# Turning V and A with VectorE and a scratch in HBM in place of TensorE, in a layer of attention, retention and a gated MLP

## The chip, the cores and the metric

The kernel runs on one core of a Trainium2 chip. The metric is the time of one launch on the device in microseconds (us), lower is better; runs are compared by their median. Engines are named as the profile names them: PE (TensorE, matmul), PEld (its weight load), DVE (VectorE), ACT (ScalarE), POOL (GpSimd) and SP (SyncE, which here issues the DMAs).

## What is computed

One layer over 256 tokens and 16 meta tokens (272 positions), 2048 wide, in float32. Cut to what matters:

```python
u = rmsnorm(h, attn_norm); proj = u @ w_in
aq, ak, av, rq, rk, rv, rg = split(proj)
# 8 attention heads: two score maps of 64 dims each, one V of 128 dims
p = softmax(q @ k.T * scale + alibi)            # for both maps
ya = (p[0] - lam * p[1]) @ av                    # A @ V
ya = rmsnorm(ya) * (1 - lam_init)
# 4 retention heads: q, k of 128 dims, V of 256 dims
yr = rmsnorm(retention(rq, rk, rv)) * silu(rg)
h = h + concat(ya, yr) @ w_out
u = rmsnorm(h, ffn_norm)
h = h + (silu(conv3(u @ w_gate)) * (u @ w_up)) @ w_down
out = rmsnorm(h)
```

Only the last 258 positions are needed as queries (3 blocks of 86, `QT`); keys come in blocks of 100, 86 and 86 (`KB`).

## The kernel before

**Tiling.** Activations lie transposed: features on the partitions, positions along the free axis. A projection of 128 features is one `gemm` (L262 to L303): 16 blocks of the contraction, three matmuls each, since weights and activations are split into a high and a low part (`whi`, `wlo`; `xhi`, `xlo`): whi with x high, whi with x low, wlo with x high (L292 to L294). That makes 48 matmuls of 258 columns (q) or 272 (k, v). An attention head is three gemms, q, k and v; a retention head is four for k, q and two halves of v, and two more for its gate.

**Weights.** A gemm's weights are one chunk of 1 MB. SP loads it into one of three buffers (`raw`, L95); ACT rounds each half of it into `whi` (L107) and DVE subtracts for `wlo` (L108), three buffers each. The next chunk is loaded into a buffer when both halves of its old chunk have been split. So the split of a chunk's second half on DVE sets when the load three chunks on is issued. SP's queue issues every DMA of this kernel's main part, in one order.

**Order.** What goes beside the gemms is a list of side tasks; `gemm` takes the next one from it (`pump`) after every quarter, every 12 matmuls. A head puts 12 tasks on the list when its gemms are written, so they run beside the gemms of the next head or the one after. The first four gemms take nothing, which leaves the list some tasks behind. Within that, the order on each engine is set by the framework's scheduler, which places instructions by its own estimate of times.

**An attention head's tasks** (`att_tasks`, L324). `scores(i)` for the three blocks of queries: four matmuls into the PSUM tile `sc`, the bias and row minimum on DVE, the exponentials on ACT, and on DVE the difference of the two maps, `A` (L367; queries on partitions, keys along the free axis). V comes out of its gemm with its features on the partitions. The value product needs keys on the partitions, of both: `vtr` (L372) turns V with 3 transposes on PE into `pv`, and DVE copies it to SBUF (`vt`, L376, L377); `atr` (L380) turns A with 6 into `pa`, and ACT and DVE copy it (`at`, L389). `av` (L393) is the value product (L398, 12 records in the trace), with its row norm; `ytr` (L408) turns the result back with PE.

**A retention head's tasks** (`ret_tasks`, L430). `scores`, then `vtr`, which turns both halves of V with 6 transposes on PE (`rv`, L456) and copies them on ACT (L459), then `av` (`ro`, L467), `stats` and `scale`.

**After that** comes the output projection (L569 to L591). There each of the 16 steps turns a tile in blocks of 32 x 32 on DVE (`hb`, L586) and stores it in four DMAs to a scratch in HBM (`hd`, L589), beside the load of a residual tile (`xres`, L571); later the rows are loaded from it. The MLP, two thirds of the kernel, follows.

Of the kernel before, what the change touches and what calls it, by code (L numbers as in the profile page):

```python
# [10 lines left out]
F32 = mybir.dt.float32  # L11
# [3 lines left out]
AF = mybir.ActivationFunctionType  # L15
ALU = mybir.AluOpType
# [3 lines left out]
P = 128  # L20
# [4 lines left out]
T = META + SEQ  # L25
Q0 = META - 2
NQ = T - Q0
QT = NQ // 3
TW = 288
XO = 32 - META  # L30
# [29 lines left out]
def trunk_kernel(ctx, tc, a, out):  # L60
    nc = tc.nc
# [90 lines left out]
    def misc(name):  # L152
        return ps1.tile([P, 512], F32, tag="misc", bufs=3, name=name)
# [145 lines left out]
    with ExitStack() as p1:  # L299
# [22 lines left out]
        late = []  # L322

        def att_tasks(h, q, k, v):  # L324
            slope = 2.0 ** (-(h + 1))
            tasks = []
            As = {}
            vt = ap_.tile([P, 3, P], F32, tag="vt", name=f"vt{h}")
# [10 lines left out]
            def scores(i):  # L339
                def f():  # L340
# [17 lines left out]
                    for m in range(2):  # L358
# [7 lines left out]
                    A = ap_.tile([QT, T], F32, tag="A", bufs=3, name=f"A{h}_{i}")  # L366
                    V.scalar_tensor_tensor(out=A[:, :nk], in0=e[:, 1, :nk], scalar=sm[:, 1:2],  # L367
                                           in1=e[:, 0, :nk], op0=ALU.mult, op1=ALU.add)
                    As[i] = A
                return f  # L370

            def vtr():  # L372
                ps = misc(f"pv{h}")
                for j, (b, e) in enumerate(KB):
                    PE.transpose(ps[:e - b, j * P:(j + 1) * P], v[:, b:e], idt)
                V.tensor_copy(out=vt[:KB[0][1], 0], in_=ps[:KB[0][1], :P])  # L376
                V.tensor_copy(out=vt[:QT, 1:3].rearrange("p a b -> p (a b)"),  # L377
                              in_=ps[:QT, P:3 * P])

            def atr():  # L380
                pa = [misc(f"pa{h}_0"), misc(f"pa{h}_1")]
                for j, (b, e) in enumerate(KB):
                    for i in range(j, 3):
                        c = (i - j) * QT + (j == 1) * NQ
                        PE.transpose(pa[j // 2][:e - b, c:c + QT], As[i][:, b:e],
                                     idt[:QT, :QT])
                for j, (b, e) in enumerate(KB):
                    c = (j == 1) * NQ
                    (V.tensor_copy if j else S.copy)(  # L389
                        out=at[j][:e - b].rearrange("p a b -> p (a b)"),  # L390
                        in_=pa[j // 2][:e - b, c:c + (3 - j) * QT])
# [25 lines left out]
            def turn():  # L417
                vtr()
                atr()

            def values():
                av()
                while late:
# [3 lines left out]
            return [prelude, scores(0), scores(1), nop, scores(2), nop, nop, turn,  # L427
                    nop, values, nop, nop]

        def ret_tasks(r, k, q, vs):  # L430
# [20 lines left out]
            def vtr():  # L451
                pv = [misc(f"rv{r}_0"), misc(f"rv{r}_1")]
                for j, (b, e) in enumerate(KB):
                    for c in range(2):
                        d = (j % 2) * 2 * P + c * P
                        PE.transpose(pv[j // 2][:e - b, d:d + P], vs[c][:, b:e], idt)  # L456
# [39 lines left out]
            return [scores, nop, vtr, nop, nop, av, nop, nop, stats, scale]  # L496
# [327 lines left out]
```

## Time and profile before

| | |
|---|---|
| median of 3 runs | 1181.58 us (1180.9 to 1181.71) |
| the profiled execution | 1180.86 us |
| its span in the profile | 1179.1 us |
| mean granted clock of PE | 0.998 of full speed |
| attention and retention stage | up to some 340 us of the span |

A row of groups in the profile reads: line, engine, operation, tile written <- tiles read, partitions x elements, type, count | busy us, mean ns of one | idle time of the engine ahead of them, and what ended it. A row of the timeline: start, duration, engine, line, operation. A row of waits: who waited <- for what: us in total, times, the longest. A row of the chain: start, duration, engine, line and count, of the chain of work that ended last. Names lose their numbers in these rows: `pa` stands for all heads' `pa5_0` and the like.

### The profile page before, as it was taken

To read this page: it belongs to the slowest core of one execution; us is meant where nothing else is said; L and a number is where in the kernel's file an instruction comes from. 1 tells how busy PE (TensorE), PEld (TensorE's weight loads), DVE (VectorE), ACT (ScalarE), POOL (GpSimd) and SP (SyncE) were. 2 spreads that over 40 slices of the span, in tenths; PEclk is the share of its full clock that TensorE was granted. 3 is DMA by queue.
4 is the path that set the end of the run, shared out by engine and by line. 5 is a ranking of instruction groups with operands and counts; after the bars stand their busy time and mean duration, and the time that the engine had idled before them with its cause. 6 is when DMAs were issued, how large, how long until landed. Compare 5 with 4: busy or idle time off the path is not lost.

```text
span 1179.1 us, 19921 instructions
## 1 busy us (share of the span) xinstructions
PE 1168.4 (99%) x8087; PEld 1094.0 (93%) x8087; DVE 803.1 (68%) x1442; ACT 561.6 (48%) x871; POOL 2.0 (0%) x7
## 2 busy tenths in 40 slices
PE   9999999999999999999999999999999999999997
PEld 8999999999999999999999999999999888888886
DVE  7898787766677677776767767677767645454544
ACT  7566665544444444444444444444444434343442
POOL 0000000000000000000000000000000000000000
PEclk9999999999999999999999999999999999999999
DMA  8543434445458776555555554455555655555552
GB/s 309 188 150 136 168 137 167 150 150 179 146 180 247 224 238 220 191 190 189 179 180 187 193 192 179 179 183 188 197 184 179 217 206 184 198 195 185 195 193 106
DMA packets 53661, 219.82 MB, mean 186 GB/s; under 512 B 21763, under 2 KB 26091, under 8 KB 28609
## 3 DMA queue, kind: packets, MB, share of 16 engines
q1 hardware_dynamic: 53280, 217.36, 52.7%
q8 instruction: 63, 1.03, 0.3%
q0 software_dynamic: 144, 1.05, 0.2%
q14 instruction: 30, 0.24, 0.1%
q10 hardware_dynamic: 144, 0.14, 0.0%
HBM read 214.34 MB, written 4.19 MB: 185 GB/s over the span
## 4 chain that ended last, share of the span: by engine, by line
PE 96%; DVE 2%; DMA 1%; issue 0%; ACT 0%; DVEq 0%; ACTq 0%
PE mm L292 17%; PE mm L293 17%; PE mm L294 17%; PE mm L288 14%; PE mm L290 7%; PE o L657 7%; PE o L658 7%; PE o L659 7%; PE po L398 1%; DMA raw<-in_w_in_dram 1%; PE ro L467 1%; DVE wlo L108 1%; PE mm L211 0%; PE mm L287 0%; PE mm L213 0%
## 5 line engine op out<-in xcount | busy, mean ns | idle before, releaser
L108 DVE TENSOR_TENSOR wlo<-raw,whi 128x1024 fp32r<-128x1024 f32 x381 | 466.2, 1224 | 244.2 <-ACT whi L107 239.0
L107 ACT CAST whi<-raw 128x1024 fp32r<-128x1024 f32 x381 | 400.1, 1051 | 480.8 <-PE mm L293 259.9
L288 PE MATMUL mm<-g,whi 128*128 128x512 f32 x704 | 249.1, 393 | 0.0
L293 PE MATMUL mm<-g,whi 128*128 128x258 f32 x704 | 199.9, 284 | 0.0
L292 PE MATMUL mm<-g,whi 128*128 128x258 f32 x704 | 199.5, 283 | 0.0
L292 PE MATMUL mm<-x,whi 128*128 128x272 f32 (+1 forms) x688 | 199.2, 290 | 0.0
L293 PE MATMUL mm<-x,whi 128*128 128x272 f32 (+1 forms) x688 | 198.9, 289 | 0.0
L294 PE MATMUL mm<-g,wlo 128*128 128x258 f32 x704 | 198.8, 282 | 0.0
L294 PE MATMUL mm<-x,wlo 128*128 128x272 f32 (+1 forms) x688 | 197.3, 287 | 1.1 <-DVE wlo L108 1.1
L290 PE MATMUL mm<-g,wlo 128*128 128x256 f32 x660 | 185.2, 281 | 0.0
L288 PEld LDWEIGHTS mm<-g,whi 128*128 128x128 f32 x704 | 132.1, 188 | 26.1
L293 PEld LDWEIGHTS mm<-g,whi 128*128 128x128 f32 x704 | 132.4, 188 | 1.9
L294 PEld LDWEIGHTS mm<-g,wlo 128*128 128x128 f32 x704 | 132.9, 189 | 0.0
L292 PEld LDWEIGHTS mm<-g,whi 128*128 128x128 f32 x704 | 132.5, 188 | 0.0
L294 PEld LDWEIGHTS mm<-x,wlo 128*128 128x128 f32 x688 | 129.7, 189 | 1.3 <-DVE wlo L108 1.3
L658 PE MATMUL o<-wlo,fhi 128*128 128x512 f32 x334 | 130.0, 389 | 0.0
L659 PE MATMUL o<-whi,flo 128*128 128x512 f32 x334 | 130.0, 389 | 0.0
L293 PEld LDWEIGHTS mm<-x,whi 128*128 128x128 f32 x688 | 129.8, 189 | 0.0
L292 PEld LDWEIGHTS mm<-x,whi 128*128 128x128 f32 x688 | 129.7, 188 | 0.0
L290 PEld LDWEIGHTS mm<-g,wlo 128*128 128x128 f32 x660 | 124.4, 189 | 0.0
L657 PE MATMUL o<-whi,fhi 128*128 128x512 f32 x334 | 117.0, 389 | 0.0
L659 PEld LDWEIGHTS o<-whi,flo 128*128 128x128 f32 x334 | 62.7, 188 | 13.0
(245 smaller groups left out, 1366.7 us busy)
## 6 DMA issues: line engine op xcount, KB each, us to landing
raw<-in_w_in_dram SPq DMA_DIRECT2D x44, 1024.0 KB, 4.7
raw<-in_w_gate_dram SPq DMA_DIRECT2D x44, 1024.0 KB
raw<-in_w_up_dram SPq DMA_DIRECT2D x44, 1024.0 KB, 4.8
raw<-in_w_down_dram SPq DMA_DIRECT2D x44, 1024.0 KB, 4.7
raw<-in_w_out_dram SPq DMA_DIRECT2D x16, 1024.0 KB, 4.8
raw<-in_w_first_dram SPq DMA_DIRECT2D x6, 512.0 KB
xres<-in_x_dram SPq DMA_DIRECT2D x16, 129.0 KB, 4.3
hd<-hb SPq DMA_DIRECT2D x64, 32.0 KB, 3.7
```

The source lines that it names most:

```text
L107: S.copy(out=hi, in_=src)
L108: V.tensor_tensor(out=lo, in0=src, in1=hi.bitcast(F32), op=ALU.subtract)
L288: PE.matmul(ps[:, :2 * n], wh, xb, start=(k == 0), stop=(k == KT - 1))
L290: PE.matmul(ps[:, :n], wl, xh, start=False, stop=False)
L292: PE.matmul(ps[:, :n], wh, xh, start=(k == 0), stop=False)
L293: PE.matmul(ps[:, :n], wh, xl, start=False, stop=False)
L294: PE.matmul(ps[:, :n], wl, xh, start=False, stop=(k == KT - 1))
L398: PE.matmul(ps[:QT, i * P:(i + 1) * P], at[j][:n, i - j], vt[:n, j], start=(j == 0), stop=(j == i))
L467: PE.matmul(y[:, c, j * QT:NQ], vt[:n, j, cs], sd[j][:n], start=(j == 0), stop=(j == 2))
L657: PE.matmul(o, ah, wh, start=start and kk == 0, stop=False)
L658: PE.matmul(o, ah, wl, start=False, stop=False)
L659: PE.matmul(o, al, wh, start=False, stop=stop and kk == 1)
```

## The change

V and A are no longer turned by PE. DVE transposes them in blocks of 32 x 32 into another tile, stores put these blocks in their turned places in a scratch in HBM, and loads fetch the turned matrix from there. V goes out in four stores (`hv`), a retention head's in eight (`rhv`), each of three blocks of A in three (`ha`; the last of the three only 22 columns wide, since a block has 86 queries); V comes back in two loads, A in three. A's and V's tiles are padded to whole blocks and their pads set to zero by POOL. The value product of a head, which was the tenth task of its own twelve, is put on `due` and runs in the fourth task of the next head's list, directly behind that head's second scores. In a retention head the loads stand in the second task, `av` in the eighth. One square on ACT of 2 x 258 takes the place of two. The tiles that this needs take the places of others (`g0`, `g1`, `k2`, `bias`).

The lines of the gemm move down by one (L293 to L295), the value product is L421 and the third split L109.

```diff
@@ -320,11 +321,31 @@
 
         nop = lambda: None
         late = []
-
-        def att_tasks(h, q, k, v):
+        due = []
+
+        def last_av():
+            while due:
+                due.pop()()
+
+
+        def turned(v, vb, hv, c):
+            V.transpose(out=vb, in_=v)
+            for i in range(4):
+                d = c * P + i * 32
+                nc.sync.dma_start(
+                    out=hv[:, d:d + 32].rearrange("(b t) f -> t b f", t=32),
+                    in_=vb[i * 32:(i + 1) * 32].rearrange("t (b f) -> t b f", f=32))
+
+        AW = (128, 192, TV)
+        Ab = [ap_.tile([96, AW[i]], F32, name=f"Ab{i}", bufs=1) for i in range(3)]
+        for A in Ab:
+            nc.gpsimd.memset(A, 0.0)
+
+        def att_tasks(h, q, k, hv):
             slope = 2.0 ** (-(h + 1))
             tasks = []
             As = {}
+            ha = dp.tile([TV, NQ], F32, name=f"ha{h}")
             vt = ap_.tile([P, 3, P], F32, tag="vt", name=f"vt{h}")
             at = [ap_.tile([P, 3 - j, QT], F32, tag=f"at{j}", name=f"at{h}_{j}")
                   for j in range(3)]
@@ -363,32 +384,34 @@
                     V.tensor_tensor(out=sm[:, 1:2], in0=sm[:, 1:2], in1=nlam[:QT], op=ALU.mult)
                     V.tensor_scalar(out=e[:, 0, :nk], in0=e[:, 0, :nk], scalar1=sm[:, 0:1],
                                     scalar2=None, op0=ALU.mult)
-                    A = ap_.tile([QT, T], F32, tag="A", bufs=3, name=f"A{h}_{i}")
-                    V.scalar_tensor_tensor(out=A[:, :nk], in0=e[:, 1, :nk], scalar=sm[:, 1:2],
-                                           in1=e[:, 0, :nk], op0=ALU.mult, op1=ALU.add)
-                    As[i] = A
+                    V.scalar_tensor_tensor(out=Ab[i][:QT, :nk], in0=e[:, 1, :nk],
+                                           scalar=sm[:, 1:2], in1=e[:, 0, :nk],
+                                           op0=ALU.mult, op1=ALU.add)
+                    As[i] = ap_.tile([P, TV], F32, tag="g1", name=f"A{h}_{i}")[:96, :AW[i]]
+                    V.transpose(out=As[i], in_=Ab[i])
                 return f
 
-            def vtr():
-                ps = misc(f"pv{h}")
+            def vload():
+                nc.sync.dma_start(out=vt[:KB[0][1], 0], in_=hv[:KB[0][1]])
+                nc.sync.dma_start(out=vt[:QT, 1:3],
+                                  in_=hv[KB[0][1]:T].rearrange("(a s) d -> s a d", s=QT))
+
+            def atr(i):
+                def f():
+                    for p in range(3):
+                        n = min(32, QT - 32 * p)
+                        c = i * QT + 32 * p
+                        nc.sync.dma_start(
+                            out=ha[:AW[i], c:c + n].rearrange("(b t) f -> t b f", t=32),
+                            in_=As[i][p * 32:p * 32 + 32].rearrange(
+                                "t (b f) -> t b f", f=32)[:, :, :n])
+                return f
+
+            def aload():
                 for j, (b, e) in enumerate(KB):
-                    PE.transpose(ps[:e - b, j * P:(j + 1) * P], v[:, b:e], idt)
-                V.tensor_copy(out=vt[:KB[0][1], 0], in_=ps[:KB[0][1], :P])
-                V.tensor_copy(out=vt[:QT, 1:3].rearrange("p a b -> p (a b)"),
-                              in_=ps[:QT, P:3 * P])
-
-            def atr():
-                pa = [misc(f"pa{h}_0"), misc(f"pa{h}_1")]
-                for j, (b, e) in enumerate(KB):
-                    for i in range(j, 3):
-                        c = (i - j) * QT + (j == 1) * NQ
-                        PE.transpose(pa[j // 2][:e - b, c:c + QT], As[i][:, b:e],
-                                     idt[:QT, :QT])
-                for j, (b, e) in enumerate(KB):
-                    c = (j == 1) * NQ
-                    (V.tensor_copy if j else S.copy)(
-                        out=at[j][:e - b].rearrange("p a b -> p (a b)"),
-                        in_=pa[j // 2][:e - b, c:c + (3 - j) * QT])
+                    nc.sync.dma_start(out=at[j][:e - b].rearrange("p a b -> p (a b)"),
+                                      in_=ha[b:e, j * QT:])
+                due.append(values)
 
             def av():
                 ps = misc(f"po{h}")
@@ -414,20 +437,16 @@
                                        in1=yhi[:, h].bitcast(F32), op0=ALU.mult,
                                        op1=ALU.subtract)
 
-            def turn():
-                vtr()
-                atr()
-
             def values():
                 av()
                 while late:
                     late.pop()()
                 late.append(ytr)
 
-            return [prelude, scores(0), scores(1), nop, scores(2), nop, nop, turn,
-                    nop, values, nop, nop]
-
-        def ret_tasks(r, k, q, vs):
+            return [prelude, scores(0), scores(1), last_av, scores(2), atr(0), atr(1), vload,
+                    atr(2), nop, nop, aload]
+
+        def ret_tasks(r, k, q, hv):
             dt_ = ap_.tile([P, 2, NQ], F32, tag="t", name=f"dk_{r}")
             nc.sync.dma_start(out=dt_[:KB[0][1], 0], in_=a["decay0"][r])
             nc.sync.dma_start(out=dt_[:QT, 1], in_=a["decay1"][r])
@@ -449,14 +468,9 @@
                                     in1=dk[j], op=ALU.mult)
 
             def vtr():
-                pv = [misc(f"rv{r}_0"), misc(f"rv{r}_1")]
-                for j, (b, e) in enumerate(KB):
-                    for c in range(2):
-                        d = (j % 2) * 2 * P + c * P
-                        PE.transpose(pv[j // 2][:e - b, d:d + P], vs[c][:, b:e], idt)
-                for j, (b, e) in enumerate(KB):
-                    d = (j % 2) * 2 * P
-                    S.copy(out=vt[:e - b, j], in_=pv[j // 2][:e - b, d:d + 2 * P])
+                nc.sync.dma_start(out=vt[:KB[0][1], 0], in_=hv[:KB[0][1]])
+                nc.sync.dma_start(out=vt[:QT, 1:3],
+                                  in_=hv[KB[0][1]:T].rearrange("(a s) d -> s a d", s=QT))
 
             def av():
                 y = st["y"] = ps1.tile([P, 2, 512], F32, tag="sc", bufs=1, name=f"ro{r}")
@@ -466,10 +480,9 @@
                         n = e - b
                         PE.matmul(y[:, c, j * QT:NQ], vt[:n, j, cs], sd[j][:n],
                                   start=(j == 0), stop=(j == 2))
-                for c in range(2):
-                    q_ = ap_.tile([P, NQ], F32, tag="A", bufs=3, name=f"rsq{r}_{c}")
-                    S.activation(out=q_, in_=y[:, c, :NQ], func=AF.Square)
-                    st[c] = q_
+                q_ = ap_.tile([P, 2, NQ], F32, tag="bias", bufs=1, name=f"rsq{r}")
+                S.activation(out=q_, in_=y[:, :, :NQ], func=AF.Square)
+                st[0], st[1] = q_[:, 0], q_[:, 1]
                 while late:
                     late.pop()()
 
@@ -493,7 +506,7 @@
                     V.tensor_tensor(out=t, in0=st["y"][:, c, :NQ], in1=st["r"], op=ALU.mult)
                     yn[r, c] = t
 
-            return [scores, nop, vtr, nop, nop, av, nop, nop, stats, scale]
+            return [scores, vtr, nop, nop, nop, nop, nop, av, nop, stats, scale]
 
         yn = {}
 
@@ -514,14 +527,17 @@
         for h in range(AH):
             q = ap_.tile([P, NQ], F32, tag="q", name=f"q{h}")
             k = ap_.tile([P, T], F32, tag="k", name=f"k{h}")
-            v = ap_.tile([P, T], F32, tag="v", name=f"v{h}")
+            v = ap_.tile([P, TV], F32, tag="v", name=f"v{h}")
+            nc.gpsimd.memset(v[:, T:], 0.0)
             ps = gemm(idx, xhi, xlo, Q0, NQ, 1)
             V.scalar_tensor_tensor(out=q, in0=ps[:, :NQ], scalar=0.125, in1=rq_,
                                    op0=ALU.mult, op1=ALU.mult)
             ps = gemm(idx + 1, xhi, xlo, 0, T, 1)
             V.tensor_tensor(out=k, in0=ps[:, :T], in1=rk_, op=ALU.mult)
             ps = gemm(idx + 2, xhi, xlo, 0, T, 1)
-            V.tensor_tensor(out=v, in0=ps[:, :T], in1=rk_, op=ALU.mult)
+            V.tensor_tensor(out=v[:, :T], in0=ps[:, :T], in1=rk_, op=ALU.mult)
+            hv = dp.tile([TV, P], F32, name=f"hv{h}")
+            turned(v, ap_.tile([P, TV], F32, tag="g0", name=f"vb{h}"), hv, 0)
             idx += 3
             q2 = ap_.tile([P, 2, NQ], F32R, tag="q2", name=f"q2_{h}")
             k2 = ap_.tile([P, 2, T], F32R, tag="k2", name=f"k2_{h}")
@@ -535,11 +551,12 @@
                 V.tensor_copy(out=k2[os, m], in_=k[hs])
                 V.tensor_tensor(out=kl[hs, m], in0=k[hs], in1=k2[hs, m].bitcast(F32),
                                 op=ALU.subtract)
-            side.extend(att_tasks(h, q2, (k2, kl), v))
+            side.extend(att_tasks(h, q2, (k2, kl), hv))
+        side.extend([nop, nop, nop, last_av])
         for kind, r in RSEQ:
             if kind == "g":
                 for c in range(2):
-                    g = ap_.tile([P, NQ], F32, tag=f"g{c}", name=f"rg{r}_{c}")
+                    g = ap_.tile([P, TV], F32, tag=f"g{c}", name=f"rg{r}_{c}")[:, :NQ]
                     ps = gemm(idx, xhi, xlo, Q0, NQ, 1)
                     V.tensor_tensor(out=g, in0=ps[:, :NQ], in1=rq_, op=ALU.mult)
                     S.activation(out=g, in_=g, func=AF.Silu)
@@ -552,14 +569,16 @@
             V.tensor_tensor(out=k, in0=ps[:, :T], in1=rk_, op=ALU.mult)
             ps = gemm(idx + 1, xhi, xlo, Q0, NQ, 1)
             V.tensor_tensor(out=q, in0=ps[:, :NQ], in1=rq_, op=ALU.mult)
-            vs = []
+            vb = ap_.tile([P, 2, TV], F32, tag="k2", name=f"rvb{r}")
+            hv = dp.tile([TV, 2 * P], F32, name=f"rhv{r}")
             for c in range(2):
-                v = ap_.tile([P, T], F32, tag="e" if c else "v", name=f"rv{r}_{c}")
+                v = ap_.tile([P, TV], F32, tag="e" if c else "v", name=f"rv{r}_{c}")
+                nc.gpsimd.memset(v[:, T:], 0.0)
                 ps = gemm(idx + 2 + c, xhi, xlo, 0, T, 1)
-                V.tensor_tensor(out=v, in0=ps[:, :T], in1=rk_, op=ALU.mult)
-                vs.append(v)
+                V.tensor_tensor(out=v[:, :T], in0=ps[:, :T], in1=rk_, op=ALU.mult)
+                turned(v, vb[:, c], hv, c)
             idx += 4
-            side.extend(ret_tasks(r, k, q, vs))
+            side.extend(ret_tasks(r, k, q, hv))
         pump(len(side))
 
         gs = [big.tile([P, 2, HK, TW], F32R, tag=f"act{i}", name=f"g{i}") for i in range(2)]
```

PE, head 5. `mm22` is head 7's k gemm, `sc6_1` the second scores of head 6, `py4` the turning back of head 4's result. Before, from the last matmuls ahead of the value product, and A's transposes further up:

```order
L385 MATMUL pa5_0_2279<-c_ident_444,A5_2_2201 100x86
L385 MATMUL pa5_0_2279<-c_ident_444,A5_1_2151 86x86
...
L294 MATMUL mm22_2370<-x1_72,wlo45_2303 128x272
L398 MATMUL po5_2318<-vt5_1931,at5_0_1932 86x128 x2
L411 MATMUL py4_2351<-c_ident_444,yo_4_1623 128x86 x3
L292 MATMUL mm22_2370<-x1_72,whi45_2302 128x272
```

Now:

```order
L293 MATMUL mm23_2500<-x0_71,whi46_2401 128x272
L366 MATMUL sc6_1_2480<-k2_6_2310,q2_6_2309 86x186
L368 MATMUL sc6_1_2480<-klz_466,q2_6_2309 86x186
L366 MATMUL sc6_1_2480<-k2_6_2310,q2_6_2309 86x186
L368 MATMUL sc6_1_2480<-klz_466,q2_6_2309 86x186
L421 MATMUL po5_2519<-vt5_2000,at5_0_2001 86x128 x2
L421 MATMUL po5_2519<-vt5_2000,at5_1_2002 86x128
L421 MATMUL po5_2519<-vt5_2000,at5_0_2001 86x128
```

The product stood in head 7's k gemm, ahead of head 6's first scores; it has moved behind head 6's second scores, into head 7's v gemm (`mm23`), and the transposes `pa5` are gone.

SP, the same place. Before, only weights stood there:

```order
L95 DMA raw24_2371<-in_w_in_dram 128x2048
L95 DMA raw25_2468<-in_w_in_dram 128x2048
L95 DMA raw26_2567<-in_w_in_dram 128x2048
L95 DMA raw27_2683<-in_w_in_dram 128x2048
L95 DMA raw28_2781<-in_w_in_dram 128x2048
```

Now (`hv6` is head 6's V, `ha5` and `at5` are head 5's A):

```order
L96 DMA raw24_2399<-in_w_in_dram 128x2048
L404 DMA ha5_1999<-A5_1_2175 32x6x32 x2
L404 DMA ha5_1999<-A5_1_2175 32x6x22
L335 DMA hv6_2302<-vb6_2303 32x9x32 x4
L96 DMA raw25_2501<-in_w_in_dram 128x2048
L395 DMA vt6_2322<-hv6_2302 100x128
L404 DMA ha5_1999<-A5_2_2265 32x9x32 x2
L404 DMA ha5_1999<-A5_2_2265 32x9x22
L396 DMA vt6_2322<-hv6_2302 86x2x128
L412 DMA at5_0_2001<-ha5_1999 100x258
L412 DMA at5_1_2002<-ha5_1999 86x172
L412 DMA at5_2_2003<-ha5_1999 86x86
```

Between two loads of weights stand now the stores and loads of V and A, on the one queue; the last block's stores are behind raw25 and behind a load that waits for hv6's stores.

DVE, between the split of raw22's first half (`wlo44`) and that of raw23's (`wlo46`), now:

```order
L109 TENSOR_TENSOR wlo44_2337<-raw22_2179,whi44_2336 128x1024
L134 SCALAR_TENSOR_TENSOR r3t_2215<-r3o_2216,ms4_2207 86x3
L332 STREAM_TRANSPOSE vb6_2303<-v6_2009 128x288
...
L109 TENSOR_TENSOR wlo45_2370<-raw22_2179,whi45_2369 128x1024
L387 SCALAR_TENSOR_TENSOR Ab2_471<-e5_2_2257,sm5_2_2258 86x272
L134 SCALAR_TENSOR_TENSOR r3t_2215<-r3o_2216,ms4_2207 86x3
L533 SCALAR_TENSOR_TENSOR q7_2329<-mm21_2333,rstd1_81 128x258
L391 STREAM_TRANSPOSE A5_2_2265<-Ab2_471 96x288
L135 TENSOR_TENSOR r3t_2215<-r3t_2215,r3o_2216 86x3
L109 TENSOR_TENSOR wlo46_2402<-raw23_2334,whi46_2401 128x1024
```

The transpose of V, which PE did, stands behind `wlo44`, and that of A's last block behind `wlo45` and the multiplication that ends head 7's q gemm.

More of the change, by code (lines that the diff above doesn't have):

```diff
@@ L29 @@
 TW = 288
+TV = 288
 XO = 32 - META
@@ L569, in trunk_kernel @@
         for j in range(KT):
-            xr = ap_.tile([P, NQ], F32, tag="g0", name=f"xres{j}")
+            xr = ap_.tile([P, TV], F32, tag="g0", name=f"xres{j}")[:, :NQ]
             nc.sync.dma_start(out=xr, in_=a["x"][:, j, Q0:T])
             ps = gemm(idx + j, yhi, ylo, 0, NQ, 1)
-            hT = ap_.tile([P, NQ], F32, tag="g1", name=f"hT{j}")
+            hT = ap_.tile([P, TV], F32, tag="g1", name=f"hT{j}")[:, :NQ]
             V.tensor_tensor(out=hT, in0=ps[:, :NQ], in1=xr, op=ALU.add)
```

## The prediction

> **What bounds the kernel now.** I read the page first: busy times of the engines, then who is waited for.
>
> ```profile
> PE 1168.4 (99%) x8087; PEld 1094.0 (93%) x8087; DVE 803.1 (68%) x1442; ACT 561.6 (48%) x871; POOL 2.0 (0%) x7
> ```
>
> TensorE (PE) is busy through the whole span of 1179.1 us. The view of waits, for PE alone, says in what it ever waits:
>
> ```profile
> PE psx L158 <- DVE warm L146: 1.6, 1, 1.6
> PE mm L294 <- DVE wlo L108: 1.1, 1, 1.1
> ```
>
> Twice: once at the start, once while the first heads are set up. So each matmul taken from PE's stream shortens the kernel by the time it holds the stream, and each wait put into the stream lengthens it. How long a matmul holds the stream is not its mean duration, because matmuls overlap. Four rows of the timeline, PE alone, give the step from one to the next:
>
> ```profile
> 89.46 0.28 PE L294 MATMUL mm<-x,wlo 128*128 128x258 f32 x1
> 93.81 0.29 PE L294 MATMUL mm<-x,wlo 128*128 128x258 f32 x1
> 93.94 0.28 PE L292 MATMUL mm<-x,whi 128*128 128x272 f32 x1
> 95.81 0.28 PE L292 MATMUL mm<-x,whi 128*128 128x272 f32 x1
> ```
>
> Between the first two lie 36 steps: 4.35/36 = 0.121 us each. Between the last two lie 15: 1.87/15 = 0.125 us. A matmul of 0.28 us holds the stream for less than half of that.
>
> **What is removed.** The transposes are these groups (lines by shape: count, then busy us and mean ns):
>
> ```profile
> L385 PE MATMUL pa<-c_ident,A 86*100 86x86 f32 x24 | 4.9, 238 | 0.0
> L375 PE MATMUL pv<-c_ident,v 128*86 128x128 f32 x16 | 3.0, 272 | 0.0
> L375 PE MATMUL pv<-c_ident,v 128*100 128x128 f32 x8 | 2.2, 272 | 0.0
> L385 PE MATMUL pa<-c_ident,A 86*86 86x86 f32 x24 | 3.2, 237 | 0.0
> L456 PE MATMUL rv<-c_ident,rv 128*86 128x128 f32 x16 | 2.6, 273 | 0.0
> L456 PE MATMUL rv<-c_ident,rv 128*100 128x128 f32 x8 | 1.5, 272 | 0.0
> ```
>
> That is 48 of A, 24 of V in the attention heads and 24 of V in the retention heads. The chain of waits (start, us) says what they hold of the stream:
>
> ```profile
> 78.15 0.33 PE pv L375 x3
> 100.45 0.45 PE pa L385 x6
> 249.21 0.66 PE rv L456 x6
> ```
>
> So 0.11 us for one of V and 0.075 for one of A: 48 x 0.075 + 24 x 0.11 + 24 x 0.11 = 3.6 + 2.64 + 2.64 = **8.9 us**. The sum of the six busy times, 17.4 us, would be wrong by the overlap.
>
> One place gives some back. The second wait of PE ends a chain over DVE:
>
> ```profile
> 52.11 0.29 DVE vt L376
> 52.75 1.24 DVE wlo L108
> 54.03 0.39 PE mm L294
> ```
>
> The copies of head 0's V (0.64 us from one start to the next row's) go, but one or two transposes of V on DVE come before that split, of about 0.5 us each (next part): up to 0.3 us more. And the three transposes of head 0's V stood before this wait, where their 0.33 us only makes PE wait longer. Off go 0.6: **-8.3 us** before any new wait.
>
> **What is added, beside other work.** DVE loses four copies in each head and gains four transposes. The nearest row of such a transpose is L586:
>
> ```profile
> L586 DVE STREAM_TRANSPOSE hb<-hT 128x256 f32<-128x256 f32 x16 | 7.1, 445 | 0.5
> L377 DVE COPY vt<-pv 86x256 f32<-86x256 f32 x8 | 3.3, 408 | 0.0
> L389 DVE COPY at<-pa 86x172 f32<-86x172 f32 x8 | 2.6, 325 | 0.2 <-ACT at L389 0.2
> L376 DVE COPY vt<-pv 100x128 f32<-100x128 f32 x8 | 2.3, 282 | 0.1
> L389 DVE COPY at<-pa 86x86 f32<-86x86 f32 x8 | 1.9, 242 | 2.2 <-PE pa L385 2.1
> ```
>
> By columns: V, 288 wide, 0.50; A, 128, 192 and 288 wide, 0.22 + 0.33 + 0.50; together 1.55 us against 0.408 + 0.325 + 0.282 + 0.242 = 1.26. DVE gets 0.3 us more to do in each head of some 21 us. The first of these windows is such a head (span; PE, PEld, DVE, ACT, POOL busy; clock, DMA share, GB/s):
>
> ```profile
> 151.00:172.00 21.00, 21.00 (x178) 21.00 (x178) 17.16 (x58) 13.25 (x33) 0.00 (x0) 1.00 0.42 152
> 360.00:380.00 20.00, 20.00 (x168) 20.00 (x167) 13.94 (x22) 10.22 (x15) 0.00 (x0) 1.00 0.74 215
> 500.00:600.00 100.00, 100.00 (x707) 94.05 (x706) 70.35 (x107) 45.96 (x62) 0.00 (x0) 1.00 0.53 189
> ```
>
> DVE's 17.2 us of 21 become 17.5: hidden, as long as the splits of the weights keep their lead. ACT and PSUM only get relief. The pads' memsets go to POOL, which is idle.
>
> DMA gets 13 stores and 5 loads per head, the stores in pieces of 128 B or less: 4 x 288 + 3 x 608 = 2976 pieces. The second window holds the same kind of store (hd, 256 pieces of 128 B each, four per 5.8 us, and xres); its share is 0.21 above the third window's, or 4.2 us of 16 engines in 20 us for some 3500 pieces: at most 0.019 us of one engine each. A head's new pieces so cost 2976 x 0.019/16 = 3.5 us, its share goes from 0.42 to about 0.6. Under a share of 0.74 weights still come on time. Nor do the weights get late here (rows in the next part): raw24, issued at 152.05, has landed by 156.8; raw22 is split from 154.18 on (wlo44), and the fourth split after it, the first of raw24, is at 169.48.
>
> **The new wait.** A's way to the value products was PE, PSUM and a copy; now it is store, completion, load, completion, all on SP's one queue. The order after shows what stands there: raw25, the first load of vt6 (which waits for hv6's stores), the three stores of A5_2, the other load of vt6, three loads at5. I place this on the old trace:
>
> ```profile
> 152.05 0.33 SPq L95 DMA_DIRECT2D raw<-in_w_in_dram  x1
> 152.94 0.29 PE L347 MATMUL sc<-klz,q 128*86 128x272 f32 x1
> 154.18 1.21 DVE L108 TENSOR_TENSOR wlo<-raw,whi 128x1024 fp32r<-128x1024 f32 x1
> 158.84 0.33 SPq L95 DMA_DIRECT2D raw<-in_w_in_dram  x1
> 159.46 0.43 DVE L519 SCALAR_TENSOR_TENSOR q<-mm,rstd 128x258 f32<-128x258 f32 x1 [0.65 <-PE mm L294]
> 169.48 1.21 DVE L108 TENSOR_TENSOR wlo<-raw,whi 128x1024 fp32r<-128x1024 f32 x1
> ```
>
> When PE needs it: from the last second-map score of head 5 (152.94) to the first value product the order after has 122 gemm matmuls (48 of 258 columns, 74 of 272) and 8 scores, 15.6 us by the steps above: 168.5. When A5_2 is there: its transpose stands behind q7's multiplication (159.46 + 0.43): 160.4. When hv6 is there: vb6's transpose stands behind wlo44 (154.18 + 1.21), so four stores go out from 155.9 to 157.7. What the stores and loads take is in the DMA rows:
>
> ```profile
> L589 SPq DMA_DIRECT2D hd<-hb x64: 302/442/1095, 348.3 to 432.8; - x64
> DMA to landing us min/median/max: 1.7/3.7/4.3
> raw<-in_w_in_dram SPq DMA_DIRECT2D x44, 1024.0 KB, 4.7
> xres<-in_x_dram SPq DMA_DIRECT2D x16, 129.0 KB, 4.3
> ```
>
> An issue holds the queue 0.44 us. A landing takes 1.7 us at least and 3.7 to 4.3 close behind a weight load (xres is issued about a microsecond behind one, and hd's stores after it). So three landings follow one another: hv6 (last issued at 157.3), A5_2's stores (the third issued 0.9 us behind the first), and at5.
> [...]
> - All at 4.3: 161.6, 162.9 + 4.3 = 167.2, + 4.3 = 171.5. PE waits 3.0 us, in each of 8 heads: 24 us.
> - By the nearest rows: hv6 and at5 have no weight load right ahead (about 2), A5_2's stores do (3.7): 159.3; A5_2 from 160.4, third at 161.3, landed 165.0; at5_0 at 167.5. A microsecond is left.
>
> I take the last, and 2 us in all for heads in which it does not hold: head 7's stores stand among the eight stores of the first retention head's V, which are 3.5 us of issue on the same queue.
>
> The retention heads' V makes the same trip with eight stores; its product stands six task slots (of 12 matmuls, some 1.5 us each) behind the loads, 9 us against a landing of 4.3 at most, so I put no wait there.
>
> [...]
>
> **The sum.** 1180.86 (the profiled execution; span 1179.1 and 1.8 around it) - 8.9 + 0.6 + 2.0 = 1174.6. The median of the runs shown, 1181.58, lies 0.7 above that execution, so I say **1175**. A measurement of this kernel tells about 0.2% from no change, here 1179.2 to 1183.9.
>
> **Rivals.**
> 1. *The round trip takes what PE gives.* All three landings at hd's median: hv6 161.0, stores from 161.4, third at 162.3, landed 166.0, at5_0 at 169.7: PE waits 1.2 us x 8 = 9.6; 1180.9 - 8.3 + 9.6 = 1182, no difference. For it speaks that 3.7 is the median of such stores; against it, that all of these had a weight load and xres ahead of them.
> 2. *Slower: PE waits for at in every head.* One mechanism, the landing of A's second trip, at the place po L421. It costs from 1.04 us per head on (8.3/8) all that was won, and from 1.33 it is slower by over 0.2%. With 4.3 for each landing it is 3.0 us: 1180.9 - 8.3 + 24 = 1196.5; half way, at 2 us, 1188.6. For it: the margin is a microsecond over three landings, and a head that waits shifts the next one's work with it, so the wait repeats. Against it: the first landing has nothing big ahead of it.
> 3. *The full gain.* No new wait, and the first heads lose nothing: 1180.9 - 8.9 = 1172.
> 4. *DMA is slow at turned pieces.* If a piece cost several times 0.019 us, the head's 3.5 us would become more than the 21 us have left, and weights would come late: four times is 14 us on top of 8.9, over 21 by 2 us per head, about 1189. hd's stores have the same pieces and speak against it. [...]
>
> **How the numbers follow.** My forecast with small waits (1172 to 1178, rival 3 in it) 0.65; rival 1 (1179 to 1184) 0.14; rival 2 0.18; rival 4 0.03. Faster 0.65, same 0.14, slower 0.21. The range from 1171.5 to 1188 leaves out the worst of rivals 2 and 4; the likeliest case alone is 1172 to 1178.
>
> **What would show it.** The waits of PE: `po` waiting for `at` under 0.3 us per head says that I am right, over 1 us rival 1 or 2, and the view of the tile ha gives the landing that did it. A wait of `mm` on wlo or whi would be rival 4 or a DVE that lost its lead. The number of PE's matmuls falls by 96; if the span shrinks by less than 8 us with no wait listed, the steps of 0.11 and 0.075 were wrong.

## The result and the profile after

The changed kernel takes 1196.26 us (median of 4 runs, 1195.22 to 1198.02) against 1181.49 for the kernel before: 1.0129 of its time, 95% interval 1.0117 to 1.0141. It is slower by 15 us; the forecast was 1175.

The page, first the busy times, then the slices of the granted clock (tenths):

```profile
span 1193.5 us, 20056 instructions
PE 1170.2 (98%) x7991; PEld 1091.9 (91%) x7991; DVE 806.1 (68%) x1450; ACT 555.3 (47%) x847; POOL 4.3 (0%) x26
PEclk9989999899999999999999999999999999999999
PE 88%; DMA 6%; DVE 3%; ACT 1%; issue 1%; SPq 1%; DVEq 0%; ACTq 0%
```

The 96 matmuls are gone, yet PE is busy longer, and DMA is on the chain that ended last. Two slices have a clock of 8. The waits of PE in the changed kernel:

```profile
PE po L421 <- DMA at<-ha: 11.5, 12, 2.8
PE psx L159 <- DVE warm L147: 1.6, 1, 1.6
PE mm L295 <- DVE wlo L109: 1.4, 1, 1.4
PE mm L212 <- ACT whi L204: 0.4, 1, 0.4
PE mm L212 <- ACT x L194: 0.2, 1, 0.2
PE ro L481 <- DMA rvt<-rhv: 0.2, 1, 0.2
```

Together 15.3 us against 2.7: 12.6 more, nearly all in front of the value products, for the loads of A. The timeline of head 5, PE alone:

```profile
174.56 0.25 PE L368 MATMUL sc<-klz,q 128*86 128x186 f32 x1
175.35 0.67 PE L421 MATMUL po<-vt,at 100*86 100x128 f32 x4 [0.54 <-DMA at<-ha]
176.99 0.89 PE L421 MATMUL po<-vt,at 86*86 86x128 f32 x6 [0.97 <-DMA at<-ha]
178.27 0.72 PE L421 MATMUL po<-vt,at 86*86 86x128 f32 x2 [0.39 <-DMA at<-ha]
```

And SP's issues ahead of it:

```profile
164.77 0.43 SPq L335 DMA_DIRECT2D hv<-vb  x1
165.50 0.50 SPq L96 DMA_DIRECT2D raw<-in_w_in_dram  x1
167.97 0.30 SPq L395 DMA_DIRECT2D vt<-hv  x1
168.36 1.30 SPq L404 DMA_DIRECT2D ha<-A  x3
169.71 0.33 SPq L396 DMA_DIRECT2D vt<-hv  x1
173.18 0.98 SPq L412 DMA_DIRECT2D at<-ha  x3
```

PE waits three times in one product, once for each load of A, though the three are issued within a microsecond (173.18, 0.98 us for the three). Over all heads the first loads cost 5.5 us, the second and third 6.0.

The clock, in windows that touch the products of heads 0, 5 and 7 (PE, PEld, DVE, ACT, POOL busy; then the granted clock):

```profile
82.00:86.00 4.00, 3.16 (x16) 3.16 (x17) 0.94 (x6) 1.44 (x8) 0.00 (x0) 0.59 0.78 266
86.00:90.00 4.00, 4.00 (x21) 4.00 (x21) 2.66 (x11) 0.75 (x4) 0.00 (x0) 0.56 0.51 124
174.00:178.00 4.00, 2.37 (x18) 1.74 (x16) 2.99 (x9) 0.22 (x1) 0.00 (x0) 1.00 0.83 255
178.00:182.00 4.00, 3.73 (x18) 3.73 (x19) 1.44 (x10) 2.96 (x12) 0.00 (x0) 0.57 0.22 66
220.00:224.00 4.00, 1.12 (x4) 0.79 (x4) 0.80 (x1) 1.26 (x2) 0.00 (x0) 0.83 0.63 180
224.00:228.00 4.00, 3.34 (x16) 3.34 (x17) 0.33 (x2) 1.24 (x7) 0.00 (x0) 0.50 0.76 210
228.00:232.00 4.00, 4.00 (x28) 3.89 (x27) 2.50 (x9) 1.05 (x1) 0.00 (x0) 0.82 0.38 126
```

After some of these waits the clock is halved. One minus the clock, times 4 us: 1.6 + 1.8 in head 0, 1.7 in head 5, 0.7 + 2.0 + 0.7 in head 7: **8.5 us** that half clock cost at most. PE waited through 1.0 us of these stretches, so 8.0 us is nearer. The timeline of head 0 shows the end of such a stretch:

```profile
88.92 0.43 PE L294 MATMUL mm<-x,whi 128*128 128x272 f32 x1
89.15 0.43 PE L295 MATMUL mm<-x,wlo 128*128 128x272 f32 x1
89.38 0.37 PE L293 MATMUL mm<-x,whi 128*128 128x272 f32 x1
89.58 0.29 PE L294 MATMUL mm<-x,whi 128*128 128x272 f32 x1
89.71 0.29 PE L295 MATMUL mm<-x,wlo 128*128 128x272 f32 x1
```

The step of a 272-column matmul goes from 0.23 to 0.13 us. So the span of 1179.1 becomes: - 8.9 (transposes) + 12.6 (waits) + 8.5 (clock) = 1191.3. The 2.2 us left (2.7 if the clock is put at 8.0) fit the edges of the 12 waits: the last matmul ahead of a wait counts as busy to its end, 0.25 us for the score at 174.56 and 0.29 for most, where the next one would have started after 0.09 to 0.13; some 0.16 us each, 2 us in all. That share is worked out, not tested.

### The profile page after: what moved, and what is told of

Its sections match the earlier page's. It is cut to its first block, busy times and chain, and to the rows that moved or that the text cites. A ratio compares the mean times of both kernels' runs of the same rounds, so it can differ in the third digit from the quotient of the medians.

```text
span 1193.5 us, 20056 instructions
## 1 busy us (share of the span) xinstructions
PE 1170.2 (98%) x7991; PEld 1091.9 (91%) x7991; DVE 806.1 (68%) x1450; ACT 555.3 (47%) x847; POOL 4.3 (0%) x26
## 4 chain that ended last, share of the span: by engine, by line
PE 88%; DMA 6%; DVE 3%; ACT 1%; issue 1%; SPq 1%; DVEq 0%; ACTq 0%
PE mm L293 15%; PE mm L294 15%; PE mm L295 14%; PE mm L289 14%; PE mm L291 7%; PE o L677 6%; PE o L676 6%; PE o L678 6%; DMA at<-ha 2%; DMA ha<-A 2%; PE po L421 1%; DVE wlo L109 1%; PE ro L481 1%; DMA rvt<-rhv 1%; DMA raw<-in_w_first_dram 1%
## 5 line engine op out<-in xcount | busy, mean ns | idle before, releaser
L109 DVE TENSOR_TENSOR wlo<-raw,whi 128x1024 fp32r<-128x1024 f32 x381 | 465.7, 1222 | 244.5 <-ACT whi L108 239.0
L293 PE MATMUL mm<-x,whi 128*128 128x272 f32 (+1 forms) x688 | 200.0, 291 | 0.0
L295 PE MATMUL mm<-x,wlo 128*128 128x272 f32 (+1 forms) x688 | 198.6, 289 | 1.4 <-DVE wlo L109 1.4
L293 PE MATMUL mm<-g,whi 128*128 128x258 f32 x704 | 199.4, 283 | 0.0
L295 PE MATMUL mm<-g,wlo 128*128 128x258 f32 x704 | 198.8, 282 | 0.0
L295 PEld LDWEIGHTS mm<-x,wlo 128*128 128x128 f32 x688 | 131.6, 191 | 1.6 <-DVE wlo L109 1.6
L295 PEld LDWEIGHTS mm<-g,wlo 128*128 128x128 f32 x704 | 132.9, 189 | 0.0
L293 PEld LDWEIGHTS mm<-g,whi 128*128 128x128 f32 x704 | 132.5, 188 | 0.0
L294 PEld LDWEIGHTS mm<-x,whi 128*128 128x128 f32 x688 | 131.7, 191 | 0.0
L293 PEld LDWEIGHTS mm<-x,whi 128*128 128x128 f32 x688 | 131.7, 191 | 0.0
L676 PEld LDWEIGHTS o<-whi,fhi 128*128 128x128 f32 x334 | 62.7, 188 | 13.0
```

Of the source, the lines that this page charges most:

```text
L109: V.tensor_tensor(out=lo, in0=src, in1=hi.bitcast(F32), op=ALU.subtract)
L293: PE.matmul(ps[:, :n], wh, xh, start=(k == 0), stop=False)
L294: PE.matmul(ps[:, :n], wh, xl, start=False, stop=False)
L295: PE.matmul(ps[:, :n], wl, xh, start=False, stop=(k == KT - 1))
L676: PE.matmul(o, ah, wh, start=start and kk == 0, stop=False)
```

## The experiments

Theory: PE waits for A's round trip, the clock falls behind some of these waits, and everything else is as predicted. The rivals stand in each expectation. "Before" below is the kernel before, run beside each.

**1. The product later.**

```diff
-            return [prelude, scores(0), scores(1), last_av, scores(2), atr(0), atr(1), vload,
-                    atr(2), nop, nop, aload]
+            return [prelude, scores(0), scores(1), nop, scores(2), atr(0), last_av,
+                    both(atr(1), vload), atr(2), nop, nop, aload]
...
-        side.extend([nop, nop, nop, last_av])
+        side.extend([nop, nop, nop, nop, nop, nop, last_av])
```

> The value product of a head runs three side tasks later (behind the next head's third scores), everything else as in the changed kernel. Theory: the whole loss is PE waiting for at, and the half clock that follows some of these waits; three tasks of 1.5 us are more than the 0.7 to 2.8 us that po waits. So PE's waits for at are under 0.5 us in all, the granted clock is back at 0.997 or more, and the time is 1172 to 1175. Rival: the round trip crowds SP's queue or the DMA engines, so that the wait only moves (to a later product, to ro, to the weights' splits): 1185 or more.

Measured: 1178.67 us against 1180.68, ratio 0.998 (0.9969 to 0.999): slightly faster than before, 4 us short of the expectation. Its waits at A, from the timeline:

```profile
80.52 0.67 PE L427 MATMUL po<-vt,at 100*86 100x128 f32 x4 [0.67 <-DMA at<-ha]
82.15 1.57 PE L427 MATMUL po<-vt,at 86*86 86x128 f32 x8 [0.96 <-DMA at<-ha]
96.81 0.67 PE L427 MATMUL po<-vt,at 100*86 100x128 f32 x4 [0.42 <-DMA at<-ha]
98.43 1.35 PE L427 MATMUL po<-vt,at 86*86 86x128 f32 x8 [0.95 <-DMA at<-ha]
```

Heads 2 to 7 no longer wait for A, as expected. Heads 0 and 1 do, for 3.0 us, and the clock was halved behind both (3.4 us lost by 2 us windows; mean granted clock 0.996). Their products did not move. In the changed kernel the scheduler had them behind the next head's third scores already, not behind the second as the task list has it: by the timeline 22 gemm matmuls behind in head 0 and 29 in head 1, and the same 22 and 29 here. Head 3's went from 25 gemm matmuls behind the next head's first scores to 60. Head 0 waited in the changed kernel too; that head 1 would was not foreseen. PE reaches its product 2.0 us sooner than there (96.39 in place of 98.39).

**2. Work in the pause.**

```diff
                     PE.matmul(ps[:QT, i * P:(i + 1) * P], at[j][:n, i - j], vt[:n, j],
                               start=(j == 0), stop=(j == i))
+                if i == 0 and h in (0, 5):
+                    fl = misc(f"fill{h}")
+                    for _ in range(2):
+                        PE.matmul(fl[:QT, :3 * P], at[0][:KB[0][1], 0],
+                                  vt[:KB[0][1], 0:1].to_broadcast([KB[0][1], 3, P]),
+                                  start=True, stop=True)
```

> In heads 0 and 5 two matmuls of 384 columns, whose result nobody reads, stand between the first product (which needs only the first load of A) and the rest (which waits for the second and third load). They make PE do 1.3 us more in each of two heads. Theory: the clock halves because PE pauses there; the filler covers the second pause, the clock after the product stays at 1.0 in heads 0 and 5 (it fell for some 7 and 4 us), and the kernel gets 4 to 5 us faster than the changed one, about 1191.5, although it does more. Rival: the clock does not depend on these pauses: it falls all the same, and the time is the changed kernel's or up to 1 us more, 1196 to 1197.

Measured: 1194.2 us, ratio 1.01 (1.0073 to 1.0126); some 2 us under the changed kernel, not 4 to 5, and their intervals overlap. Windows at heads 0, 1 and 5:

```profile
80.00:84.00 4.00, 3.99 (x27) 3.04 (x27) 3.84 (x10) 2.81 (x10) 0.00 (x0) 1.00 0.88 267
84.00:88.00 4.00, 4.00 (x35) 4.00 (x35) 3.77 (x24) 1.98 (x7) 0.11 (x1) 1.00 0.60 135
94.00:98.00 4.00, 1.02 (x6) 0.80 (x7) 3.13 (x13) 3.29 (x8) 0.00 (x0) 0.85 0.57 125
98.00:102.00 4.00, 4.00 (x20) 4.00 (x20) 2.66 (x10) 1.99 (x10) 0.00 (x0) 0.50 0.70 236
180.00:184.00 4.00, 4.00 (x36) 4.00 (x35) 3.38 (x19) 3.40 (x13) 0.00 (x0) 1.00 0.35 111
```

In heads 0 and 5 the clock stays at 1.00, as the theory has it. But PE comes to head 1's product the sooner, waits there 2.5 and 1.0 us, and the clock falls there, to 0.85 and then 0.50 in these windows; over the span its mean is 0.992, against 0.991 in the changed kernel. What a filled pause saved was lost at the next load that was late. It shows where the clock falls, not what a fall costs; that is read from the windows.

**3. V alone, and 4. no transposes at all.** The third is the changed kernel with A's part as before, `atr` that of the kernel before. The second diff is the fourth kernel's, against the kernel before:

```diff
-            return [prelude, scores(0), scores(1), last_av, scores(2), atr(0), atr(1), vload,
-                    atr(2), nop, nop, aload]
+            return [prelude, scores(0), scores(1), last_av, scores(2), nop, nop, vload,
+                    nop, nop, nop, aload]
...
             def aload():
-                for j, (b, e) in enumerate(KB):
...
+                atr()
                 due.append(values)
```

```diff
-            vt = ap_.tile([P, 3, P], F32, tag="vt", name=f"vt{h}")
-            at = [ap_.tile([P, 3 - j, QT], F32, tag=f"at{j}", name=f"at{h}_{j}")
-                  for j in range(3)]
+            vt, at = flat[:, :3 * P].rearrange("p (a b) -> p a b", a=3), [
+                flat[:, :(3 - j) * QT].rearrange("p (a b) -> p a b", b=QT) for j in range(3)]
...
             def vtr():
-                ps = misc(f"pv{h}")
...
+                pass
```

> V goes by DVE and HBM as in the changed kernel, in attention and retention heads; A is turned by PE, PSUM and copies as before, at the place where the changed kernel loads it; the product stands where the changed kernel has it. Theory: V's trip has enough ahead of it, only A's does not. So po waits for nothing, the 48 transposes of V save 5.3 us less about 0.6 in the first heads: 1176 to 1177. Rival: any round trip costs PE a wait, V's too, or the product's new place does: 1181 or more.

> The kernel before with all 96 transposes of V and A and their copies left out; the products read a zeroed tile instead of the turned V and A, so they compute something else. Nothing else is added. It measures what the transposes hold of PE's stream. Theory: 8.9 us by the steps in the chain (0.075 and 0.11 us each), and perhaps another 1 us at the one wait of the first heads, since DVE loses copies there: 1171.5 to 1173. Rival: the steps overstate it, and the removed transposes are worth 6 to 7 us only: 1174.5 to 1175.5.

Measured: V alone 1176.61 us against 1180.68, ratio 0.9962 (0.9948 to 0.9977). That is within the expectation. None of the attention heads' products waits for a load; PE waits 0.6 us once for a load of the retention's V. Without transposes 1170.35, ratio 0.991 (0.9895 to 0.9925): 10.3 us less, and 1.2 us under the expected range. The wait of 1.1 us in the first heads is gone from its list of waits, but three short ones at the very start, 0.8 us together, have come. So some 10 us are the transposes', a microsecond more than the steps gave; the interval, 8.9 to 12.4 us, allows both. The removed work was sized rightly to within about that microsecond, V's trip alone is hidden, and the loss comes with A's.

**5. A alone.** V's part as before, on PE; A and the product as in the changed kernel.

```diff
-            side.extend(att_tasks(h, q2, (k2, kl), hv))
+            side.extend(att_tasks(h, q2, (k2, kl), v))
...
-            return [prelude, scores(0), scores(1), last_av, scores(2), atr(0), atr(1), vload,
+            return [prelude, scores(0), scores(1), last_av, scores(2), atr(0), atr(1), vtr,
```

> The other half: A goes by DVE and HBM as in the changed kernel, with the product at the changed kernel's place; V is turned by PE, PSUM and copies as before, in attention and retention heads. V's stores and loads are gone from SP's queue, so the stores of A's last block no longer stand behind a load that waits for V's stores (1.4 us later than A was ready, in head 5). Theory: that delay was part of the wait, the slow landing of A's second and third load the rest. The first loads come 1 to 1.5 us sooner, the waits for the first load nearly vanish (5.5 us of 11.5), those for the second and third shrink but do not vanish, and the clock falls once or twice: waits of 3 to 6 us, clock loss 2 to 5 us, against 3.6 saved: 1181 to 1189. Rival: V's traffic has no part in it, the waits stay at 11 us and the clock loss at 8.5: 1196 + 5 = 1200 or more.

Measured: 1191.41 us, ratio 1.0089 (1.0075 to 1.0104), outside the theory's range and the rival's. The timeline:

```profile
100.49 0.89 PE L424 MATMUL po<-vt,at 86*86 86x128 f32 x6 [1.52 <-DMA at<-ha]
101.76 0.45 PE L424 MATMUL po<-vt,at 86*86 86x128 f32 x2 [0.38 <-DMA at<-ha]
...
176.59 0.89 PE L424 MATMUL po<-vt,at 86*86 86x128 f32 x6 [1.13 <-DMA at<-ha]
177.89 0.45 PE L424 MATMUL po<-vt,at 86*86 86x128 f32 x2 [0.41 <-DMA at<-ha]
```

The waits for the first loads shrink to 1.5 us in all (from 5.5), as expected: V's trip, on DVE and on the queue, had delayed them. Those for the second and third, on the 86-row loads, were expected to shrink and grow to 8.2 (from 6.0): they have a cause of their own.

**6. Loads of 112 and 96 rows.**

```diff
-        AW = (128, 192, TV)
+        AW = (128, 224, TV)
+        LD = ((0, 112), (KB[1][0], KB[1][0] + 96), (KB[2][0], KB[2][0] + 96))
...
-                nc.sync.dma_start(out=vt[:KB[0][1], 0], in_=hv[:KB[0][1]])
-                nc.sync.dma_start(out=vt[:QT, 1:3],
-                                  in_=hv[KB[0][1]:T].rearrange("(a s) d -> s a d", s=QT))
+                for j, (b, e) in enumerate(LD):
+                    nc.sync.dma_start(out=vt[:e - b, j], in_=hv[b:e])
...
-                for j, (b, e) in enumerate(KB):
+                for j, (b, e) in enumerate(LD):
                     nc.sync.dma_start(out=at[j][:e - b].rearrange("p a b -> p (a b)"),
```

> The changed kernel, with loads of V and A that fetch 112 and 96 rows in place of 100 and 86 (the rows behind are pads or are not read; A's middle block is padded to 224 columns for it, and V's second load becomes two). In the changed kernel the second and third load of A land 1.3 to 1.9 us behind one another though they are issued 0.33 us apart, and PE waits 6.0 us for them of 11.5 in all. [...] Then the second and third load land with the first: PE waits once per head instead of two or three times, 2 to 5 us in all instead of 11.5, the clock falls less often (0 to 3.4 us instead of 8.5), and the time is 1177 to 1186. Rival: they land late because the next weight load of 1 MB is issued right behind them: nothing changes, 1195 to 1197.

> e1_later (product three tasks later) with the same loads of 112 and 96 rows, V and A of all heads by DVE and HBM. Theory: PE waits for A at most once, in the first heads, and its clock does not fall; what is left is the kernel without any of the 96 transposes (1170.4) with some 0.2 to 0.4 us at the first heads and at the retention's V: 1170.5 to 1173, faster than before by 0.65 to 0.85%. Rival: the waits in heads 0 and 1 come from the first heads' crowded DVE and SP, not from the loads, and stay: 1176 to 1179 as e1_later.

Measured: in the changed kernel 1190.94 us, ratio 1.0077 (1.0061 to 1.0092); with the later product 1178.29, 0.9971 (0.9961 to 0.9981). Both miss their theory's range; the first lies between it and the rival's, the second in the rival's, 1176 to 1179. The timeline of the first:

```profile
95.95 1.22 PE L421 MATMUL po<-vt,at 100*86 100x128 f32 x9 [1.72 <-DMA at<-ha]
111.75 1.78 PE L421 MATMUL po<-vt,at 100*86 100x128 f32 x12 [3.18 <-DMA ha<-A]
131.54 1.55 PE L421 MATMUL po<-vt,at 100*86 100x128 f32 x12 [1.05 <-DMA at<-ha]
154.41 1.85 PE L421 MATMUL po<-vt,at 100*86 100x128 f32 x12 [1.94 <-DMA at<-ha]
219.99 3.09 PE L421 MATMUL po<-vt,at 100*86 100x128 f32 x12 [3.34 <-DMA at<-ha]
```

One wait per product; what follows runs through. So what holds the second and third loads back in the changed kernel is not the weight load behind them, which is still there (in head 5 issued at 175.06, behind the loads at 173.77; in the changed kernel at 174.26, behind 173.18). Loads of 86 rows came with a second or third wait in six of the eight products, loads of 96 rows with none. Why a load of 86 rows lands later was not shown, nor that the rows are the whole of it: V's loads and A's middle block changed with them.

The first loads gained little: heads 1 and 2, which had not waited, now wait 1.7 and 3.2 us, and the sum of waits for A, 12.8 us, is no smaller than the changed kernel's. PE comes to these two products 4.2 and 2.7 us sooner than in the changed kernel (94.23 and 108.57 in place of 98.39 and 111.23), their loads are issued only 1.3 and 0.3 us sooner (93.82 and 107.66 in place of 95.08 and 107.91). The gain of 5 us is fewer waits (7 for 12), and less half clock (10.2 us for 17.1, some 3.4 us of time). The scheduler also ordered SP anew: in head 5, which no longer waits, A's last stores (166.57) now go out ahead of V's loads (168.90), so that head does not show the rows alone. With the product later, heads 0 to 2 still wait 0.3, 1.6 and 3.2 us, as the rival had it for the first two, and the time is that of experiment 1 (1178.29 and 1178.67). Why head 2 waits there, which it did not in experiment 1, was not settled beyond this.

**7. A of the first heads by PE.** In the first kernel for heads 0 and 1 (loads of 100 and 86 rows), in the second for heads 0 to 2 (112 and 96), each with the later product.

```diff
+                    if h < 2:
+                        As[i] = Ab[i][:QT]
+                        return
                     As[i] = ap_.tile([P, TV], F32, tag="g1", name=f"A{h}_{i}")[:96, :AW[i]]
...
             def aload():
+                if h < 2:
+                    aturn()
+                    due.append(values)
+                    return
```

> As e1_later (product three tasks later), but A of heads 0 and 1, the only heads whose products still waited there (3.0 us, and 3.4 us of half clock behind it), is turned by PE as before; V and A of the other six heads go by DVE and HBM. Theory: PE then waits for no load of A, the clock stays at 0.998 or more, and of e1_later's 1178.7 the 6.4 us of waits and clock go while 0.9 us of transposes come back: 1172 to 1174, faster than the kernel before by 0.6 to 0.7%. Rival: the first heads have something else that holds them (DVE, SP's queue), and the wait moves to head 2: 1176 to 1179.

> Product three tasks later, loads of 112 and 96 rows (as e10_rows_later), and A of heads 0, 1 and 2, whose products were the only ones that still waited there (5.2 us in all, and 1.7 us of half clock), turned by PE as before; A of the other five heads and all of V by DVE and HBM. Theory: no wait for A is left and the clock does not fall; the time is that of the kernel without any transposes, 1170.4, and 3 x 0.45 us of A's transposes and up to 1 us of small waits at the retention's V and the first heads: 1171.7 to 1173.5, and so 1 to 3 us faster than e8_two_by_pe (1174.8). Rival: the trip through HBM has a cost besides waits and clock (DMA, DVE), and it stays at e8_two_by_pe's time or above: 1174.5 or more.

Measured: 1174.82 us against 1180.95, ratio 0.9947 (0.9933 to 0.9961), 0.8 us above its range, and **1172.82** against 1180.62, ratio 0.9932 (0.9918 to 0.9946), within its range. In the first, one product (head 7's) still waits 0.6 us for A and the retention's V 0.5. All of PE's waits in the last kernel:

```profile
PE psx L159 <- DVE warm L147: 1.6, 1, 1.6
PE mm L212 <- ACT whi L204: 1.4, 1, 1.4
PE mm L295 <- DVE wlo L109: 0.9, 1, 0.9
```

No wait for A is left, and the mean granted clock is 0.998, as before the change. This version beats both kernels, by 7.8 us the one before. It is 2.5 us above the kernel with no transposes, 1.35 of which are the A's of three heads, by the steps. The second kernel differs from the first in the rows and in head 2; which of the two brought its 2 us was not separated.

## Why the prediction was wrong, by its own steps

- **What bounds the kernel, and what is removed (8.9 us):** right, and if anything a microsecond low. Leaving all transposes out gave 10.3 us, of which the waits that went and came make 0.3.
- **The work added to DVE and the DMA engines:** right in size. V's transpose was put at 0.50 us and A's at 0.22, 0.33 and 0.50; a row of the changed kernel has 0.47 for the widest. In the window of 21 us from 156 on DVE is busy for 17.5 us, as predicted, and the DMA share is 0.57 (about 0.6 predicted). Weights hardly came later than before: PE's one wait for a split was 1.4 us, in the first heads, where it had been 1.1.

```profile
L391 DVE STREAM_TRANSPOSE A<-Ab 96x288 f32<-96x288 f32 x8 | 3.7, 466 | 0.0
```

- **The new wait, "By the nearest rows ... A microsecond is left":** this step failed, twice. First, it had head 5's first load landed 14.6 us behind the last score of its third block (152.94 to 167.5). That score starts at 158.79 in the changed kernel, and PE went on at 175.35, 16.6 us behind it; PE was ready after 16.0, where 15.6 was predicted. The stores of A's last block went out at 168.36, 9.6 us behind the score in place of 7.5. Ahead of them on SP stood the load of V, which waited for V's stores: V's last store was issued 6.0 us behind the score, where 4.4 was taken (V's transpose itself starts 4.0 us behind the score on DVE, at 162.76, where 2.5 was taken), and the load that waits for it went out 3.2 us after that (164.77 to 167.97), not the 2 taken because hv6 and at5 were said to "have no weight load right ahead"; raw25 went out 0.7 us behind V's last store. A's stores took 3.9 (169.23, the third, to 173.18; predicted 3.7), the load 2.2 (predicted about 2). This is head 5; the first loads of the other heads were not followed in this way. Second, it stopped at "at5_0": the second and third load were not counted, and were 6.0 of the 11.5 us. The sum's term for new waits, 2.0 us, stood for heads like head 7, which alone waited 3.5 us; over all heads it was 11.5.
- **The price of a wait:** the prediction took each wait at its length ("from 1.04 us per head on"). No term had the clock, which by the windows cost some 8 us more on 12.6. The mechanism of rival 2 came true, at its place; that its time of 1196.5 was met is luck, since its composition was not: 24 us of waits were assumed, 12.6 of waits, 8.0 to 8.5 of clock and some 2 of edges came. That the kernel would be 8 us faster with the waits and without the halving is not shown: of the four executions of experiment 5's kernel the one with a mean clock of 0.997 took 1191.64 us, the one with 0.993 1190.86, though 0.004 of the span is 4.8 us (the end of the span can make some of it: its last 5.2 us in the kernel before and 4.8 in the changed one are at half clock). A PE that is slowed may wait less at the next product; that was not followed.
- **"`po` waiting for `at` under 0.3 us per head says that I am right":** it is 1.4 per head.

## What to carry to other kernels

A round trip through HBM behind an engine that never waits must be timed to its last load, at the place where the scheduler puts the consumer, and with every load's shape: here products waited up to three times with loads of 86 rows, and once at most with loads of 96. Price a pause of PE above its length: here 12.6 us of waits came with some 8 us lost at half clock. Where the first iterations still wait when the rest no longer do, keep the old way for them alone.

## What the runs showed of the hardware

- The clock was halved behind some pauses and not behind others of the same length. In the changed kernel head 3 waited 1.34 and 0.87 us and kept its clock, head 4 0.28 and 1.08; head 0 waited 0.53 and 1.24, head 5 0.54, 0.97 and 0.39, head 7 2.82 and 0.72, and lost it. The losses come in two sizes, 3.4 us behind heads 0 and 7 and 1.7 behind head 5, that is 6.8 or 3.4 us at half speed (the second row is the stretch around head 3's waits):

```profile
82.70:89.53 6.83, 6.69 (x31) 6.69 (x32) 3.15 (x14) 1.81 (x10) 0.00 (x0) 0.50 0.63 192
126.00:136.00 10.00, 7.72 (x62) 7.09 (x61) 6.54 (x28) 5.29 (x18) 0.00 (x0) 1.00 0.56 184
178.27:181.69 3.42, 3.42 (x16) 3.42 (x17) 1.13 (x8) 2.65 (x12) 0.00 (x0) 0.50 0.17 42
222.65:229.47 6.82, 5.93 (x27) 5.60 (x28) 1.28 (x7) 1.24 (x7) 0.00 (x0) 0.50 0.64 184
```

- Neither the longest wait nor their sum tells which way it goes: head 3's two, 2.21 us together, are longer than head 5's three, 1.90, and its longest, 1.34, is longer than head 5's, 0.97. What decides it was not shown; no kernel moved a pause to try it.
- In the changed kernel PE went on 1.3 to 1.9 us later behind a load of 86 rows than behind the load ahead of it (in head 5 at 175.35, 176.99 and 178.27), issued 0.33 us apart; with loads of 96 rows no product waited a second time.
